# Mixing stage and MLP: high weight parts times high and low activation parts in one 512-column matmul, the two halves of the bank added at eviction

## The chip, the cores and the metric

The kernel runs as one program on one core of a Trainium2 chip. The metric is the device time of one execution in microseconds (us). The kernel before was timed three times. One more execution was recorded by the hardware profiler, and all rows below come from that one. In the text TensorE is PE, its weight loads are PEld, VectorE is DVE, ScalarE is ACT, GpSimd is POOL and SyncE, which issues most DMAs, is SP.

## The reference

One decoder layer on 256 tokens of width 1024, all in fp32:

```python
h = rmsnorm(x, g_pre_mix)
cb, cc, cv, q, k, v, qm, ga, gb, gc = split(h @ w_in)        # 7 x 512 and 3 x 1024 columns
y_a = (cb * causal_dwconv(cc * cv, conv_mix_w)) @ w_conv_out
y_b = moba_attention(heads(q), heads(k), heads(v), rel_bias) @ w_attn_out   # 8 heads of 64, causal
y_c = memory_attention(qm, rmsnorm(mem, g_mem), w_mem_kv) @ w_mem_out       # 4 heads of 128, 256 tokens
merged = sigmoid(ga + b0) * y_a + sigmoid(gb + b1) * y_b + sigmoid(gc + b2) * y_c
x = x + rmsnorm(merged @ w_out, g_post_mix)
h = rmsnorm(x, g_pre_ffn)
a, g = split(causal_dwconv(h @ w_up, ffn_conv_w, ffn_conv_b))               # 2 x 2816 columns
x = x + rmsnorm((gelu(a) * g) @ w_down, g_post_ffn)
```

## The kernel before

**Products in parts.** Every fp32 operand of a large product is split into a high part, rounded to fp32r (a 4-byte type that PE streams in one pass), and a low part, the remainder. A product is the sum of three: high times high, high weight times low activation, low weight times high activation. Weights arrive by DMA on SP into `raw` (1 MB, three buffers). `split_until` makes the parts of a *piece* of 128x1024 numbers: ACT writes `wh` (line 191), DVE writes `wl` (line 192). There are five buffers of pieces, and a piece is split three pieces before PE uses it. Activations are kept transposed, as `hT`, `cT`, `oT`, `omT` and `h2T`, each with a high and a low half: index 0 and 1 of the second axis.

**Blocks.** `blocks` computes 128 output columns for all 256 tokens: the result has the columns on the partitions and the 256 tokens along the bank. `mm_cols` (lines 205 to 210) issues three matmuls of 256 columns for every 128 rows of the weights (a *k-tile*): 8 k-tiles for products with `hT` and `h2T`, 4 for those with `cT`, `oT`, `omT`. Two blocks share one PSUM bank, and an `evac` function then takes both at once. `bank` has four buffers (tag `mm`), `acc` four more for long accumulations.

**Stages.** After the memory branch's keys and values, the mixing stage runs the blocks of q and k (`q_evac`, `k_evac`), then attention heads with the generator `fill` between them: memory q, the short convolution's C, V and B (`conv_evac`), and the 24 steps of `merges`, where `gate` turns two blocks into tanh values and `branch` multiplies two blocks of a branch's output by them. Then comes the output product `po` with `w_out`, with 512-column matmuls whose moving operand is the weight part (`mm_ktile`, line 216). `residual` normalises and adds (`post_norm`), turns the sum `x1` with PE transposes, and makes `h2T`. In the MLP, `up` computes two blocks of the gate half and two of the other half for each of eleven chunks, scales them by the second norm's factor `r2s`, convolves, applies GELU and splits the result `f`; the product with `w_down` accumulates in `pf` by line 216, one chunk behind. The factor depends on the token, which lies along the free axis of a block, so it is spread over all partitions by a matmul of `ones` with a diagonal (`diagonals`, `spread`).

**Order.** Each engine works its queue in order. A scheduler orders the instructions by due times while the program is built. In `residual`, in the first chunk and at the very end (`manual_schedule`), the order is that of the code. `both_blocks` does the first two blocks of the MLP with all high activation parts first.

Of the kernel before, what the change touches and what calls it, by code (L numbers as in the profile page):

```python
# [19 lines left out]
P = 128  # L20
# [35 lines left out]
def trunk(ctx, tc, x, mem, rel_bias, g_pre_mix, g_post_mix, g_pre_ffn, g_post_ffn, g_mem, w_in, b_gate,  # L56
# [235 lines left out]
    def blocks(nb, a, evac):  # L292

        p, wh, wl = None, None, None
        for b in range(nb):
# [11 lines left out]
            yield  # L307

    def both_blocks(a):

        ws = [weights(hold=i > 0) for i in range(2)]
        d = [p[:, :S] for p in acc("ft")]
        for k in range(KT):
            for i, (wh, wl) in enumerate(ws):
                nc.tensor.matmul(d[i], wh[:, k], a[:, 0, k], start=(k == 0), stop=False)
                nc.tensor.matmul(d[i], wl[:, k], a[:, 0, k], start=False, stop=False)  # L316
        for i, (wh, _) in enumerate(ws):
            for k in range(KT):
                nc.tensor.matmul(d[i], wh[:, k], a[:, 1, k], start=False, stop=(k == KT - 1))  # L319
        return d  # L320

    def run(gen):
        for _ in gen:
            pass

    def to_parts(dst, scale=1.0):
        return lambda b, p: hilo(dst[:, 0, b:b + 2], dst[:, 1, b:b + 2], two(p), scale)

# [114 lines left out]
    def q_evac(b, p):  # L443
        for j, r in enumerate(HEAD):
            hi, src = q2[r, b:b + 2, j], two(p)[r]
            nc.scalar.activation(hi, src, AF.Copy, scale=DH ** -0.5)
            nc.vector.scalar_tensor_tensor(q2[HEAD[1 - j], b:b + 2, j], src, DH ** -0.5, f32(hi), op0=ALU.mult,
                                           op1=ALU.subtract)

    def k_evac(b, p):  # L450
        for j, r in enumerate(HEAD):
            hi, src = k2[r, b:b + 2, j], two(p)[r]
# [96 lines left out]
    def conv_evac(b, p):  # L549
        y = wk.tile([P, 2, S], F32, tag="y", name="y", bufs=YB)  # L550
        for i in range(2):
            nc.scalar.activation(y[:, i], z[:, b + i], AF.Copy, scale=cw[:, 8 + b + i:9 + b + i])
            conv_tail(y[:, i], z[:, b + i], cw[:, b + i:b + i + 1], cw[:, 4 + b + i:5 + b + i])
        nc.vector.tensor_tensor(y, two(p), y, ALU.mult)
        hilo(cT[:, 0, b:b + 2], cT[:, 1, b:b + 2], y)
# [3 lines left out]
    def gate(q, n):  # L559
        sg = wk.tile([P, 2 * S], F32, tag="y", name="sg", bufs=YB)  # L560
        merged[q, n] = sg

        def evac(b, p):
            for i in range(2):
                c = 8 * n + 2 * q + i
                nc.scalar.activation(sg[:, i * S:(i + 1) * S], p[:, i * S:(i + 1) * S], AF.Tanh, scale=0.5,
                                     bias=bgh[:, c:c + 1])

        return blocks(2, hT, evac)

    def branch(q, n):
        def evac(b, p):
# [4 lines left out]
            if n == 2:  # L577
                mg = merged["mg"]
                hilo(mg[:, 0, 2 * q:2 * q + 2], mg[:, 1, 2 * q:2 * q + 2], two(total), 0.5)

        return blocks(2, (cT, oT, omT)[n], evac)

    def fill():
        yield from blocks(4, hT, to_parts(qm))
        yield from blocks(4, hT, lambda b, p: nc.scalar.activation(z[:, b:b + 2], two(p), AF.Copy))
        yield from blocks(4, hT, lambda b, p: nc.vector.tensor_tensor(z[:, b:b + 2], two(p), z[:, b:b + 2], ALU.mult))
        yield from blocks(4, hT, conv_evac)
        merged["mg"] = sb.tile([P, 2, KT, S], F32R, tag="C", name="mg")
# [64 lines left out]
    def residual():  # L653
# [17 lines left out]
        r2.append(rstd_full(x1[:, 1], "r2"))  # L671
        dg2.append(diagonals(r2))


    def up(c, f, b0):
# [3 lines left out]

        def evac(half, u, p):  # L680
            v = wk.tile([P, 2, S], F32, tag="y", name="v", bufs=YB)[:, :n]
            if not r2s:
                r2s.append(spread(dg2[0], "r2s"))
# [13 lines left out]
        for half in (1, 0):  # L697
            u = wk.tile([P, 2 * S], F32, tag="y", name="u", bufs=YB)[:, :n * S]
            res.append(u)
            if c == 0 and half:  # L700
                late.append((half, u, both_blocks(h2T)))
                continue
            for _ in blocks(n, h2T, lambda b, p: late.append((half, u, p))):
                for item in late:
                    evac(*item)
                late.clear()
        g, a = res
# [69 lines left out]
```

## Time and profile before

| | |
|---|---|
| three timed runs | 461.5, 462.3, 462.58 us; median 462.3 us |
| the profiled execution | 459.3 us, of which the profiler's span is 457.5 us |
| granted TensorE clock over the span | 0.998 of 2.4 GHz |
| HBM read | 80.91 MB, 179 GB/s over the span |

The span is the time from the first to the last instruction in the trace; 1.8 us lie around it. The trace's own time lies 3.0 us under the median of the timed runs. A matmul row's duration reaches to its modelled end and overlaps the next rows, so the pace of PE is read from the distance between starts.

### The profile page before, as it was taken

The page shows a single profiled execution, that of the slowest core. Times are in us where ns is not written, and L with a number is a line of the kernel's source. Part 1 is how long each engine was busy: PE and PEld are TensorE (multiplying, and loading weights), DVE is VectorE, ACT ScalarE, POOL GpSimd, SP SyncE. Part 2 cuts the span into 40 slices and gives each one's busy share as a digit, 9 for nine tenths or more (in the row PEclk, how much of TensorE's full clock was granted, in tenths as well). Part 3 has the DMA queues.
Part 4 walks back from the last instruction along what each step waited for, and adds up shares of the span by engine and source line. Part 5 has one row for each costly group of instructions (what it writes and reads, how often), then busy time and mean ns, then how long its engine had stood idle before and what let it go on. Part 6 is the DMA issues. An engine that isn't in the chain of part 4 may idle for free.

```text
span 457.5 us, 8130 instructions
## 1 busy us (share of the span) xinstructions
PE 447.3 (98%) x3263; PEld 422.5 (92%) x3263; DVE 329.7 (72%) x524; ACT 259.1 (57%) x419; POOL 17.6 (4%) x45
## 2 busy tenths in 40 slices
PE   8999999999999999999999899999999999999993
PEld 5798999999999999999998699989999999999982
DVE  4696769759766676495466579987787787787864
ACT  5976556547465555454445467665565565565641
POOL 3330000000000000000000200000000000000001
PEclk9999999999999999999999999999999999999999
DMA  8989654544626526545958136555555555635402
GB/s 252 358 273 300 213 183 141 176 152 132 192 87 198 171 64 213 184 140 185 332 194 263 41 134 234 186 185 185 184 185 183 185 185 184 188 134 144 180 1 93
DMA packets 67890, 82.50 MB, mean 180 GB/s; under 512 B 2064, under 2 KB 60914, under 8 KB 67852
## 3 DMA queue, kind: packets, MB, share of 16 engines
q1 hardware_dynamic: 67100, 79.73, 52.5%
q0 software_dynamic: 464, 1.20, 0.9%
q10 hardware_dynamic: 288, 1.05, 0.7%
q8 instruction: 25, 0.41, 0.4%
q14 instruction: 13, 0.11, 0.1%
HBM read 80.91 MB, written 1.06 MB: 179 GB/s over the span
## 4 chain that ended last, share of the span: by engine, by line
PE 93%; DMA 3%; DVE 1%; issue 1%; ACT 1%; POOL 0%; SPq 0%; POOLq 0%; DVEq 0%; ACTq 0%
PE ft L210 21%; PE ft L209 21%; PE ft L208 21%; PE pf L216 13%; PE po L216 5%; PE pmv L216 2%; DMA raw<-in_w_in_dram 2%; PE pv L216 2%; PE po L221 2%; PE tp L272 1%; PE at L221 1%; DMA rows<-in_g_mem_dram 1%; DVE wl L192 0%; PE ft L319 0%; PE ft L316 0%
## 5 line engine op out<-in xcount | busy, mean ns | idle before, releaser
L191 ACT ACTIVATE wh<-raw 128x1024 fp32r<-128x1024 f32 (+1 forms) x147 | 151.4, 1035 | 152.5 <-PE ft L209 105.0
L192 DVE TENSOR_TENSOR wl<-raw,wh 128x1024 fp32r<-128x1024 f32 (+1 forms) x147 | 174.9, 1195 | 79.1 <-ACT wh L191 77.6
L210 PE MATMUL ft<-hT,wl 128*128 128x256 f32 x384 | 108.6, 283 | 0.0
L209 PE MATMUL ft<-hT,wh 128*128 128x256 f32 x384 | 108.6, 283 | 0.0
L208 PE MATMUL ft<-hT,wh 128*128 128x256 f32 x384 | 108.6, 283 | 0.0
L208 PE MATMUL ft<-h2T,wh 128*128 128x256 f32 x328 | 92.9, 283 | 0.0
L210 PE MATMUL ft<-h2T,wl 128*128 128x256 f32 x328 | 92.8, 283 | 0.0
L209 PE MATMUL ft<-h2T,wh 128*128 128x256 f32 x328 | 92.8, 283 | 0.0
L210 PEld LDWEIGHTS ft<-hT,wl 128*128 128x128 f32 x384 | 73.7, 192 | 0.1
L209 PEld LDWEIGHTS ft<-hT,wh 128*128 128x128 f32 x384 | 73.6, 192 | 0.1
L208 PEld LDWEIGHTS ft<-hT,wh 128*128 128x128 f32 x384 | 73.6, 192 | 0.1
L208 PEld LDWEIGHTS ft<-h2T,wh 128*128 128x128 f32 x328 | 62.9, 192 | 0.4
L209 PEld LDWEIGHTS ft<-h2T,wh 128*128 128x128 f32 x328 | 62.9, 192 | 0.3
L210 PEld LDWEIGHTS ft<-h2T,wl 128*128 128x128 f32 x328 | 62.9, 192 | 0.1
L216 PE MATMUL pf<-wh,f 128*128 128x512 f32 x176 | 49.2, 390 | 0.0
L216 PEld LDWEIGHTS pf<-wh,f 128*128 128x128 f32 x176 | 32.3, 188 | 6.1
L216 PE MATMUL pf<-wl,f 128*128 128x512 f32 x88 | 27.5, 390 | 0.0
L694 ACT ACTIVATE u<-v,fw 128x256 f32<-128x256 f32 x44 | 24.0, 589 | 4.0 <-DVE v L686 4.0
L688 DVE TENSOR_TENSOR v<-ft,r2s 128x512 f32<-128x512 f32 (+1 forms) x23 | 14.8, 644 | 10.5 <-PE ft L210 10.5
L216 PEld LDWEIGHTS pf<-wl,f 128*128 128x128 f32 x88 | 16.5, 188 | 3.6
L547 DVE SCALAR_TENSOR_TENSOR u<-v,fw,u 128x254 f32<-128x254 f32 x44 | 19.7, 478 | 0.1
L546 DVE SCALAR_TENSOR_TENSOR u<-v,fw,u 128x255 f32<-128x255 f32 x44 | 19.5, 478 | 0.3 <-ACT u L694 0.3
(190 smaller groups left out, 618.4 us busy)
## 6 DMA issues: line engine op xcount, KB each, us to landing
raw<-in_w_in_dram SPq DMA_DIRECT2D x24, 1024.0 KB, 5.1
raw<-in_w_up_dram SPq DMA_DIRECT2D x20, 1024.0 KB, 5.2
raw<-in_w_down_dram SPq DMA_DIRECT2D x22, 512.0 KB, 3.3
raw<-in_w_out_dram SPq DMA_DIRECT2D x8, 512.0 KB, 5.2
raw<-in_w_mem_kv_dram SPq DMA_DIRECT2D x8, 256.0 KB, 6.2
raw<-in_w_mem_kv_dram SPq DMA_DIRECT2D x2, 1024.0 KB, 8.2
raw<-in_w_in_dram SPq DMA_DIRECT2D x4, 512.0 KB
raw<-in_w_conv_out_dram SPq DMA_DIRECT2D x4, 512.0 KB
```

The source lines that it names most:

```text
L191: nc.scalar.activation(hi, v, AF.Copy)
L192: nc.vector.tensor_tensor(lo, v, f32(hi), ALU.subtract)
L208: nc.tensor.matmul(dst, wh[:, k], ah[:, k], start=(k == 0), stop=False)
L209: nc.tensor.matmul(dst, wh[:, k], al[:, k], start=False, stop=False)
L210: nc.tensor.matmul(dst, wl[:, k], ah[:, k], start=False, stop=(k == kt - 1))
L216: nc.tensor.matmul(d, a, w[:, c:c + 512], start=(first and w is wh and a is ah), stop=(last and a is al))
L221: nc.tensor.matmul(dst, a[i], b[j], start=(first and n == 0), stop=(last and n == 2))
L272: nc.tensor.transpose(p[:, t * P:(t + 1) * P], src[:, t, k * P:(k + 1) * P], ident)
L546: nc.vector.scalar_tensor_tensor(t[:, 1:], src[:, :S - 1], w1, t[:, 1:], op0=ALU.mult, op1=ALU.add)
L547: nc.vector.scalar_tensor_tensor(t[:, 2:], src[:, :S - 2], w0, t[:, 2:], op0=ALU.mult, op1=ALU.add)
L688: nc.vector.tensor_tensor(v, two(p)[:, :n], twice(r2s[0])[:, :n], ALU.mult)
L694: nc.scalar.activation(d, v[:, i], AF.Identity, bias=bb, scale=w2)
```

## The change

- `mm_wide` replaces `mm_cols` in all blocks but those of the memory keys. For each k-tile it issues one matmul of 512 columns, `wh` against the high and the low activation part (two runs of 256 columns, 8 k-tiles apart in SBUF, or 4), and one of 256 columns, `wl` against the high part, into the first half of the bank. A block now fills a bank, and two blocks no longer share one.
- `add_up` evicts a block: ACT copies the second half of the bank to SBUF (`t`, two buffers; in the MLP tag `e`, four buffers), then DVE adds the first half to it. The `evac` functions now read that sum in SBUF. C's blocks go straight into `z`; `gate` works in place; `branch` needs a buffer of tag `y` that it did not need before.
- The second norm's factor of the first 128 tokens is multiplied into `xs` before the transposes, a copy of `x1` scaled per partition. So after eviction only the other 128 tokens are multiplied by `r2s`, in SBUF, and the diagonal and its spreading matmul are needed for one token tile.
- `both_blocks` puts the products with low activation parts into the second half of its banks. The tile `rows` moves into `misc`, the diagonals share the buffer of `junk`.

```diff
+    def mm_wide(p, wh, wl, a):
+        kt = wh.shape[1]
+        for k in range(kt):
+            nc.tensor.matmul(p, wh[:, k], a[:, :, k], start=(k == 0), stop=False)
+            nc.tensor.matmul(p[:, :S], wl[:, k], a[:, 0, k], start=False, stop=(k == kt - 1))
+
+    def add_up(dst, p, tag="t", bufs=2):
+        t = wk.tile([P, S], F32, tag=tag, name="t", bufs=bufs)
+        nc.scalar.activation(t, p[:, S:], AF.Copy)
+        nc.vector.tensor_tensor(dst, p[:, :S], t, ALU.add)
...
+    def wide_blocks(nb, a, evac, dst=None):
+        y, wh, wl = None, None, None
+        for b in range(nb):
...
+            p = bank("ft")
+            mm_wide(p, wh[:, :, at:at + P], wl[:, :, at:at + P], a)
...
+            if b % 2 == 0:
+                y = wk.tile([P, 2, S], F32, tag="y", name="y", bufs=YB) if dst is None else dst[:, b:b + 2]
+            add_up(y[:, b % 2], p)
+            if b % 2:
+                evac(b - 1, y)
+            yield
...
-                nc.tensor.matmul(d[i], wh[:, k], a[:, 1, k], start=False, stop=(k == KT - 1))
+                nc.tensor.matmul(d[i][:, S:], wh[:, k], a[:, 1, k], start=False, stop=(k == KT - 1))
...
-        yield from blocks(4, hT, lambda b, p: nc.scalar.activation(z[:, b:b + 2], two(p), AF.Copy))
-        yield from blocks(4, hT, lambda b, p: nc.vector.tensor_tensor(z[:, b:b + 2], two(p), z[:, b:b + 2], ALU.mult))
+        yield from wide_blocks(4, hT, lambda b, y: None, z)
+        yield from wide_blocks(4, hT, lambda b, y: nc.vector.tensor_tensor(z[:, b:b + 2], y, z[:, b:b + 2], ALU.mult))
...
+        xs = wk.tile([P, 1, D], F32, tag="pT", name="xs", bufs=2)
+        nc.vector.tensor_scalar_mul(xs[:, 0], x1[:, 0], r2[0])
         for k in range(KT):
-            turn(tps[k], x1, 0, k)
+            turn(tps[k], xs, 0, k)
...
-            if isinstance(p, list):
-                for i in range(n):
-                    nc.vector.tensor_tensor(v[:, i], p[i], r2s[0], ALU.mult)
-            else:
-                nc.vector.tensor_tensor(v, two(p)[:, :n], twice(r2s[0])[:, :n], ALU.mult)
+            for i, p in enumerate(ps_):
+                add_up(v[:, i], p, "e", EB)
+            vt = v[:, :, P:]
+            nc.vector.tensor_tensor(vt, vt, r2s[0][:, None, :].broadcast_to([P, n, P]), ALU.mult)
```

**How it moves instructions.** The first place is PE's queue at the end of the product with `w_out`: `po00` and `po01` are the two halves of the first token tile, `po10` and `po11` those of the second. Before, the last rows of the first tile and the first two of the second:

```order
L216 MATMUL po00_2907<-wl_2980,mg_1575 128x512
L216 MATMUL po00_2907<-wh_2979,mg_1575 128x512
L216 MATMUL po01_2908<-wh_2963,mg_1575 128x512
L216 MATMUL po01_2908<-wh_2979,mg_1575 128x512
L216 MATMUL po01_2908<-wl_2980,mg_1575 128x512
L216 MATMUL po01_2908<-wh_2979,mg_1575 128x512
L216 MATMUL po10_2909<-wh_2929,mg_1575 128x512
L216 MATMUL po11_2910<-wh_2929,mg_1575 128x512
```

The same place now, again up to the first rows that belong to the second tile alone:

```order
L229 MATMUL po10_2700<-wh_2720,mg_1474 128x512
L229 MATMUL po00_2698<-wl_2755,mg_1474 128x512
L229 MATMUL po01_2699<-wl_2755,mg_1474 128x512
L229 MATMUL po00_2698<-wh_2754,mg_1474 128x512
L229 MATMUL po00_2698<-wh_2770,mg_1474 128x512
L229 MATMUL po01_2699<-wh_2754,mg_1474 128x512
L229 MATMUL po01_2699<-wh_2770,mg_1474 128x512
L229 MATMUL po11_2701<-wh_2720,mg_1474 128x512
L229 MATMUL po10_2700<-wl_2721,mg_1474 128x512
L229 MATMUL po00_2698<-wl_2771,mg_1474 128x512
L229 MATMUL po01_2699<-wl_2771,mg_1474 128x512
L229 MATMUL po11_2701<-wl_2721,mg_1474 128x512
```

Three matmuls of the second tile now stand ahead of the first tile's last ones; 24 used to follow, 21 do now.

The second place is DVE's queue in `residual`, from the norm of the second token tile on (`yo` is the row times the gain, `x1` the sum, `dg` the diagonal). Before:

```order
L619 TENSOR_TENSOR yo_3088<-po11_2910,gains_2904 128x512
L622 SCALAR_TENSOR_TENSOR x1_3019<-yo_3088,ro_3099,x_sb_72 128x256 x2
L622 SCALAR_TENSOR_TENSOR x1_3019<-yo_3088,ro_3099,x_sb_72 128x512
L669 SCALAR_TENSOR_TENSOR h2T_3020<-tp_3076,par_96,h2T_3020 128x256 x2
L669 SCALAR_TENSOR_TENSOR h2T_3020<-tp_3077,par_96,h2T_3020 128x256 x2
```

And now:

```order
L690 TENSOR_SCALAR xs_2871<-x1_2810,r2_2839 128x1024
L648 TENSOR_TENSOR yo_2881<-po10_2700,gains_2695 128x512
L648 TENSOR_TENSOR yo_2881<-po11_2701,gains_2695 128x512
L651 SCALAR_TENSOR_TENSOR x1_2810<-yo_2881,ro_2892,x_sb_72 128x256 x2
L651 SCALAR_TENSOR_TENSOR x1_2810<-yo_2881,ro_2892,x_sb_72 128x512
L700 SCALAR_TENSOR_TENSOR h2T_2811<-tp_2867,par_95,h2T_2811 128x256 x2
```

The scaling of the first tile, which waits for its second norm factor, stands ahead of the second tile's two rows `yo`, which stood behind no such wait.

The third place is DVE's queue after the last block of the MLP (`v` the evicted block, `u` its convolution, line 709 the product of the two halves, `f` the low part of the result, of which the second is needed by PE's last matmuls). Before, from the eviction of the last block, ft_5024:

```order
L688 TENSOR_TENSOR v_5049<-ft_5024,r2s_3242 128x256
L547 SCALAR_TENSOR_TENSOR u_4984<-v_5014,fw_855,u_4984 128x254
L227 TENSOR_TENSOR f_4905<-u_4944,f_4905 128x256
L546 SCALAR_TENSOR_TENSOR u_5019<-v_5049,fw_855,u_5019 128x255
L547 SCALAR_TENSOR_TENSOR u_5019<-v_5049,fw_855,u_5019 128x254
L709 TENSOR_TENSOR u_5019<-u_5019,u_4984 128x256
L227 TENSOR_TENSOR f_4983<-u_5019,f_4983 128x256
```

And now, from the eviction of the last block, ft_4634 (lines 578 and 579 are the convolution, 753 the product):

```order
L223 TENSOR_TENSOR v_4651<-ft_4634,t_4652 128x256
L578 SCALAR_TENSOR_TENSOR u_4599<-v_4621,fw_822,u_4599 128x255
L723 TENSOR_TENSOR v_4651<-v_4651,r2s_3048 128x128
L753 TENSOR_TENSOR u_4564<-u_4564,u_4531 128x256
L579 SCALAR_TENSOR_TENSOR u_4599<-v_4621,fw_822,u_4599 128x254
L578 SCALAR_TENSOR_TENSOR u_4629<-v_4651,fw_822,u_4629 128x255
L240 TENSOR_TENSOR f_4530<-u_4564,f_4530 128x256
L579 SCALAR_TENSOR_TENSOR u_4629<-v_4651,fw_822,u_4629 128x254
L753 TENSOR_TENSOR u_4629<-u_4629,u_4599 128x256
L240 TENSOR_TENSOR f_4598<-u_4629,f_4598 128x256
```

Ten rows stand from the last block's eviction to the last `f`, where seven stood, and the eviction itself waits for ACT's copy.

## Rows read from the trace of the kernel before

**Rows 1.** The page's first part: busy time of each engine, its share of the span, its instructions.

```profile
PE 447.3 (98%) x3263; PEld 422.5 (92%) x3263; DVE 329.7 (72%) x524; ACT 259.1 (57%) x419; POOL 17.6 (4%) x45
```

**Rows 2.** The longest entry in the list of PE's waits over the span: who was waited for, us in total, times, longest. The two entries that follow lie in the first 5 us.

```profile
PE tp L272 <- DVE x L622: 1.7, 2, 1.5
```

**Rows 3.** The groups of the first of the three matmuls of `mm_cols` (line 208) by activation, shape and count; behind the bar busy us and mean ns of one. The groups with cT and oT have 32 each, as the one with omT.

```profile
L208 PE MATMUL ft<-hT,wh 128*128 128x256 f32 x384 | 108.6, 283 | 0.0
L208 PE MATMUL ft<-h2T,wh 128*128 128x256 f32 x328 | 92.9, 283 | 0.0
L208 PE MATMUL ft<-omT,wh 128*128 128x256 f32 x32 | 8.9, 283 | 0.0
L208 PE MATMUL ft<-h2T,wx 128*128 128x256 f32 x8 | 2.3, 283 | 0.0
```

**Rows 4.** Timeline of PE in a chunk of the MLP: start, us, operation. The first three are `pf` matmuls of 512 columns in one unbroken stretch, the last two the second and the sixtieth of an unbroken run of 256-column matmuls.

```profile
339.73 1.07 PE L216 MATMUL pf<-wh,f 128*128 128x512 f32 x4
340.63 0.62 PE L216 MATMUL pf<-wl,f 128*128 128x512 f32 x2
341.09 1.07 PE L216 MATMUL pf<-wh,f 128*128 128x512 f32 x4
...
343.01 0.28 PE L209 MATMUL ft<-h2T,wh 128*128 128x256 f32 x1
...
349.97 0.28 PE L210 MATMUL ft<-h2T,wl 128*128 128x256 f32 x1
```

**Rows 5.** Timeline of PE at a head's output: six matmuls, three of 512 columns and three of 256 columns that write two separate runs of 128 columns of the bank, and the start of the next.

```profile
89.21 1.22 PE L221 MATMUL po<-pT,vk 128*128 128x512 f32 x6
90.26 0.28 PE L208 MATMUL ft<-hT,wh 128*128 128x256 f32 x1
```

**Rows 6.** Groups of instructions by line and shape, the nearest kin of those that the change adds: busy us, mean ns of one.

```profile
L566 ACT ACTIVATE sg<-ft,bgh 128x256 f32<-128x256 f32 x24 | 9.9, 464 | 0.1
L688 DVE TENSOR_TENSOR v<-ft,r2s 128x512 f32<-128x512 f32 x19 | 13.1, 690 | 9.9 <-PE ft L210 9.9
L688 DVE TENSOR_TENSOR v<-ft,r2s 128x256 f32<-128x256 f32 x4 | 1.7, 423 | 0.6 <-PE ft L210 0.6
L191 ACT ACTIVATE wh<-raw 128x1024 fp32r<-128x1024 f32 x139 | 146.6, 1059 | 148.5 <-PE ft L209 105.0 <-issue 15.8 <-PE pf L216 14.2
L192 DVE TENSOR_TENSOR wl<-raw,wh 128x1024 fp32r<-128x1024 f32 x139 | 169.5, 1224 | 77.0 <-ACT wh L191 75.6
L414 DVE TENSOR_SCALAR xn<-x_sb,rx 128x1024 f32<-128x1024 f32 x2 | 1.5, 752 | 0.8 <-POOL rx L244 0.8
```

**Rows 7.** Busy time of each engine in four stretches: from:to, length, busy us and instructions of PE, PEld, DVE, ACT and POOL, granted TensorE clock, DMA share, GB/s. They are attention with its filling, the merges, the first two chunks of the MLP, and its steady part.

```profile
70.00:140.00 70.00, 70.00 (x581) 69.61 (x580) 52.15 (x122) 41.10 (x81) 0.00 (x0) 1.00 0.45 145
140.00:237.00 97.00, 97.00 (x809) 96.87 (x809) 61.87 (x83) 50.02 (x83) 0.00 (x0) 1.00 0.57 189
268.00:303.00 35.00, 35.00 (x273) 34.02 (x272) 30.98 (x48) 22.26 (x31) 0.00 (x0) 1.00 0.61 209
303.00:439.00 136.00, 136.00 (x964) 128.34 (x963) 106.34 (x156) 77.42 (x106) 0.00 (x0) 1.00 0.51 171
```

**Rows 8.** The same four stretches for line 208 alone: one instruction is one k-tile of a block.

```profile
70.00:140.00 70.00, 47.43 (x168) 32.07 (x168) 1.00 0.45 145
140.00:237.00 97.00, 69.88 (x248) 47.37 (x248) 1.00 0.57 189
268.00:303.00 35.00, 22.40 (x79) 15.16 (x80) 1.00 0.61 209
303.00:439.00 136.00, 72.49 (x258) 49.28 (x257) 1.00 0.51 171
```

**Rows 9.** Timeline of `residual`: first DVE (`yo` of the second tile's two halves, then its `x1`), then PE's transposes of the first and of the second tile, then POOL's last step of the first tile's second norm factor `r` and of the second tile's first, `ro`. In square brackets the idle time before and who ended it.

```profile
258.56 0.69 DVE L619 TENSOR_TENSOR yo<-po,gains 128x512 f32<-128x512 f32 x1 [1.71 <-ACT junk L239]
259.92 0.69 DVE L619 TENSOR_TENSOR yo<-po,gains 128x512 f32<-128x512 f32 x1 [0.67 <-ACT junk L239]
260.91 1.54 DVE L622 SCALAR_TENSOR_TENSOR x<-yo,ro,x_sb 128x256 f32<-128x256 f32 x3 [0.30 <-POOL ro L244]
...
258.92 1.03 PE L272 MATMUL tp<-ident,x 128*128 128x128 f32 x8
261.45 0.83 PE L272 MATMUL tp<-ident,x 128*128 128x128 f32 x4 [1.50 <-DVE x L622]
...
258.17 0.57 POOL L244 TENSOR_TENSOR r<-ms,mhalf 128x1 f32<-128x1 f32 x1
...
260.31 0.57 POOL L244 TENSOR_TENSOR ro<-ms,mhalf 128x1 f32<-128x1 f32 x1
```

**Rows 10.** Timeline after the first blocks of the MLP: PE's spreading of the norm factor and the next matmul.

```profile
271.63 0.60 PE L260 MATMUL sp<-dg,ones 128*128 128x128 f32 x4
272.00 0.36 PE L208 MATMUL ft<-h2T,wh 128*128 128x256 f32 x1
```

**Rows 11.** Timeline of the end of the MLP: PE's first `pf` matmul after the last block and the row of four with the eighteenth behind that first one; DVE's eviction of the last block; ACT's high part of the last `f`.

```profile
439.31 0.63 PE L216 MATMUL pf<-wh,f 128*128 128x512 f32 x2
...
442.97 1.07 PE L216 MATMUL pf<-wh,f 128*128 128x512 f32 x4
...
439.51 0.42 DVE L688 TENSOR_TENSOR v<-ft,r2s 128x256 f32<-128x256 f32 x1
...
442.62 0.42 ACT L225 ACTIVATE f<-u 128x256 fp32r<-128x256 f32 x1 [0.49 <-DVE u L709]
```

More of the change, by code (lines that the diff above doesn't have):

```diff
@@ L451, in k_evac @@
         for j, r in enumerate(HEAD):
-            hi, src = k2[r, b:b + 2, j], two(p)[r]
+            hi, src = k2[r, b:b + 2, j], p[r]
             nc.scalar.activation(hi, src, AF.Copy)
@@ L455, in k_evac @@
             nc.vector.tensor_copy(k2[HEAD[1 - j], b:b + 2, j], f32(hi))
-    run(blocks(4, hT, q_evac))
-    run(blocks(4, hT, k_evac))
+    run(wide_blocks(4, hT, q_evac))
+    run(wide_blocks(4, hT, k_evac))
     fw = const.tile([P, 2, 4 * NFB], F32, name="fw")
@@ L578, in evac @@
                 mg = merged["mg"]
-                hilo(mg[:, 0, 2 * q:2 * q + 2], mg[:, 1, 2 * q:2 * q + 2], two(total), 0.5)
-        return blocks(2, (cT, oT, omT)[n], evac)
+                hilo(mg[:, 0, 2 * q:2 * q + 2], mg[:, 1, 2 * q:2 * q + 2], total, 0.5)
+        return wide_blocks(2, (cT, oT, omT)[n], evac)
     def fill():
-        yield from blocks(4, hT, to_parts(qm))
-        yield from blocks(4, hT, lambda b, p: nc.scalar.activation(z[:, b:b + 2], two(p), AF.Copy))
-        yield from blocks(4, hT, lambda b, p: nc.vector.tensor_tensor(z[:, b:b + 2], two(p), z[:, b:b + 2], ALU.mult))
-        yield from blocks(4, hT, conv_evac)
+        yield from wide_blocks(4, hT, to_parts(qm))
+        yield from wide_blocks(4, hT, lambda b, y: None, z)
+        yield from wide_blocks(4, hT, lambda b, y: nc.vector.tensor_tensor(z[:, b:b + 2], y, z[:, b:b + 2], ALU.mult))
+        yield from wide_blocks(4, hT, conv_evac)
         merged["mg"] = sb.tile([P, 2, KT, S], F32R, tag="C", name="mg")
@@ L671, in residual @@
         r2.append(rstd_full(x1[:, 1], "r2"))
-        dg2.append(diagonals(r2))
+        dg = wk.tile([P, P], F32, tag="junk", name="dg", bufs=1)
+        nc.vector.tensor_scalar_mul(dg, ident, r2[1])
+        dg2.append(dg)
     def up(c, f, b0):
@@ L678, in up, with evac @@
         res, late = [], []
-        def evac(half, u, p):
+        def evac(half, u, ps_):
             v = wk.tile([P, 2, S], F32, tag="y", name="v", bufs=YB)[:, :n]
             if not r2s:
-                r2s.append(spread(dg2[0], "r2s"))
-            if isinstance(p, list):
-                for i in range(n):
-                    nc.vector.tensor_tensor(v[:, i], p[i], r2s[0], ALU.mult)
-            else:
-                nc.vector.tensor_tensor(v, two(p)[:, :n], twice(r2s[0])[:, :n], ALU.mult)
+                p = bank("sp")
+                nc.tensor.matmul(p[:, :P], ones, dg2[0], start=True, stop=True)
+                r2s.append(const.tile([P, P], F32, tag="rs", name="r2s"))
+                nc.vector.tensor_copy(r2s[0], p[:, :P])
+            for i, p in enumerate(ps_):
+                add_up(v[:, i], p, "e", EB)
+            vt = v[:, :, P:]
+            nc.vector.tensor_tensor(vt, vt, r2s[0][:, None, :].broadcast_to([P, n, P]), ALU.mult)
             for i in range(n):
@@ L702, in up @@
                 continue
[L703 to L706, printed above, removed]
+            ps_, w = [], None
+            for i in range(n):
+                if w is None:
+                    w, at = weights(), 0
+                ps_.append(bank("ft"))
+                mm_wide(ps_[-1], w[0][:, :, at:at + P], w[1][:, :, at:at + P], h2T)
+                at += P
+                if at == w[0].shape[2]:
+                    w = None
+            late.append((half, u, ps_))
+            for item in late:
+                evac(*item)
+            late.clear()
         g, a = res
```

35 lines of the change are left out of this document (19 added, 16 removed).

## The prediction, made before the changed kernel was run

> **What bounds the kernel now.** I read the page's first part first: PE is busy for 447.3 of 457.5 us, and a chain of weight loads runs beside it [rows 1]. Busy is not yet bound, since a matmul row overlaps the next. So the second view is the list of PE's waits: the longest entry is 1.7 us, in `residual`, and the few others lie at the start [rows 2]. Between start and end PE has work nearly always, and the other engines are less than three quarters busy. What shortens PE's own stream shortens the kernel, as long as PE goes on not waiting.
>
> The third view is PE's pace. From 339.73 to 341.09 six matmuls of 512 columns start, 226.7 ns each. From 343.01 to 349.97 there are 58 steps of 256 columns in 6.96 us, 120.0 ns each [rows 4]. The difference of 106.7 ns for 256 columns is 2.4 columns a ns, the full clock; granted is 1.00 in every stretch [rows 7]. What remains at either width is 13.3 ns per matmul. Three matmuls of 256 take 360.0 ns, one of 512 and one of 256 take 346.7 ns: the columns are the same, one fixed cost is saved.
>
> The Trainium skill, in "TensorE: Matmul & The Clock Gate", section Back-to-back issue gap, gives N/2.4 + 2.5 ns for a warm isolated gap, 109.2 and 215.8 ns here. The trace disagrees, with 120.0 and 226.7 ns. By the page's 2.5 ns the term below would be 2.0 instead of 10.9 us.
>
> **PE's stream.** Line 208 ran for 384 k-tiles of `hT`, 328 + 8 of `h2T` and 3 x 32 of `cT`, `oT`, `omT` [rows 3]: 816 k-tiles, and each loses one matmul. 816 x 13.3 ns = **10.9 us saved**. The `memT` blocks and `both_blocks` keep their count. No row has a moving operand in two runs of 256. The bounds are 240 ns for it (two passes of 120.0 ns, nothing saved) and 226.7 ns (a matmul of 512 like `pf`). I take 226.7 ns, since six matmuls of which three write two runs take 1.05 us [rows 5], and 3 x 226.7 + 3 x 120.0 ns is 1.04 us: two runs cost nothing on the output side.
>
> The spreading of the norm factor took 0.37 us from its start to the next matmul's [rows 10], for four rows; one is left, **0.3 us saved**.
>
> **Eviction.** The 816 k-tiles make 114 blocks (48 + 42 of 8, 24 of 4), and two more come from `both_blocks`: 116 copies on ACT and 116 adds on DVE. Nearest to the copy is the tanh of 256 columns from PSUM, 464 ns; nearest to the add is the product of 256 columns with one operand in PSUM, 423 ns [rows 6]. That is 53.8 us on ACT and 49.1 us on DVE; the MLP's products from PSUM of 512 columns (690 ns) shrink to 256 columns in SBUF. None of it lies on PE's path while a bank is free in time. A block of 8 k-tiles takes 8 x 346.7 ns = 2.8 us, and with four banks three blocks lie between a bank's end and its next use: 8.3 us of cover, 4.2 us for blocks of 4. A copy behind one split on ACT and an add behind one split on DVE need 1.06 + 0.46 + 1.22 + 0.42 = 3.2 us [rows 6].
>
> So it depends on whether DVE keeps up in a stretch [rows 7, 8]. The k-tiles of a stretch give its blocks, and 13.3 ns each of PE time saved. Attention: 168 k-tiles are 21 blocks; 52.2 + 21 x 0.423 = 61.0 us in 70.0 - 2.2 us, 90%. Merges: 248 k-tiles, 24 blocks of 4 and 19 of 8; 61.9 + 43 x 0.423 = 80.1 us in 97.0 - 3.3 us, 85%. Steady MLP: 258 k-tiles, 32 blocks; 106.3 + 32 x 0.423 us, less 0.27 us (690 - 423 ns) for most of the 19 products of 512 columns [rows 6], some 115 us in 136.0 - 3.4 us, 87%. First chunks of the MLP: 79 k-tiles, 10 blocks and the two of `both_blocks`; 31.0 + 12 x 0.423 us, less some 1.6 us for smaller products, 34.5 us in 35.0 - 1.1 us. Only there is DVE full. Its work can spill into the next stretch, but the in-order queue holds adds behind splits, and the bank of the first whole block is given back only after the spread factor has been copied. I count the queue through: PE starts the fifth bank user about 0.3 us before that add ends. **0.3 us**, between 0 and 2.0 us. For attention I put **0.3 us**, between 0 and 3.0 us: DVE has 6.8 us to spare, but each softmax hangs on several steps in order. The merges and the steady MLP I put at nothing: three banks' time covers them; if that cover went, each late bank would cost PE what it is late.
>
> **`residual`.** PE's wait of 1.50 us comes from DVE's `x1` of the second tile [rows 9]. Now `xs` stands ahead of both `yo`. It needs the factor `r`, ready at 258.17 + 0.57 = 258.74 us; three matmuls of the second tile ahead of the first tile's end push it by 3 x 0.227 to 259.42 us. `xs` is kin to the 752 ns scaling of 1024 columns [rows 6]: until 260.2. Two `yo` of 0.69 us, started 0.60 apart, end at 261.45 instead of 260.61 us, and `x1`, which started at 260.91 for POOL's `ro`, starts at 261.45. **0.5 us lost**, between 0 (no push, then `yo` ends before `ro`) and 1.2 us. The transposes of the first tile start later by 1.3 us, inside the 1.5 us that PE waited anyway.
>
> **The end.** The first `pf` row after the last block starts at 439.31 us; the nineteenth, which needs the high part of the last `f`, at 439.31 + 18 x 0.227 = 443.39 us. It was ready at 442.62 + 0.42 = 443.04 us [rows 11]: 0.35 us to spare. Now the eviction is a copy (0.46 us) and an add (0.42 us) where one product of 0.42 us stood, then a product of 128 columns (some 0.3 us, an estimate from 423 ns at 256), and the DVE queue puts a convolution row of the block before between each two of these. Counted through by the order, from the block's end: the copy ends at 0.5, the add behind a convolution row at 1.3, the product behind another at 1.9, ACT's own step at 2.5, two convolution rows at 3.8, GELU at 4.3, the product of the halves at 4.75, the last high part at 5.2 us. It was 3.5 us before, and 0.35 us of that difference are to spare; the third `f`, due earlier, makes PE wait for some 0.3 us already, which is part of the same loss. **1.3 us lost**, between 0.5 (one step more on the chain, less the slack) and 1.9 us.
>
> **Sum.** -10.9 - 0.3 + 0.3 + 0.3 + 0.5 + 1.3 = -8.8 us. Against the trace's own 459.3 us (span 457.5 and 1.8 around it) that is 450.5 us. The three timed runs have a median of 462.3 us, 3.0 above it; against that it is **453.5 us**, which I give.
>
> **Rivals.**
> 1. *The fixed cost is not saved.* The two-run operand restarts at the border, or the 13.3 ns belong to something that stays. At 240 ns for the wide matmul nothing is saved, and the losses of 2.1 us (0.3 + 0.3 + 0.5 + 1.3, less 0.3) stay: 464.4 us. For it: no row shows such an operand. Against: the same 13.3 ns at both widths, and two runs at full pace on the output side. The Trainium skill, in "PSUM — Partial Sum Buffer", Specifications (TRN2), says that a non-contiguous pattern slows matmuls significantly; the two-run output of rows 5 disagrees. Chance 5%.
> 2. *Slower: banks come back late in the merges.* Blocks of 4 k-tiles leave 4.2 us of cover. With the gated product and the sum (512 columns, 0.69 us each) and both splits ahead, the way is 3.2 + 1.4 = 4.6 us. If that is the rule and a `y` buffer is waited for as well, each of the 24 branch blocks makes PE wait; at 0.5 us that is 12 us, 465.5 us. It decides from 9.7 us in all, 0.40 us per branch block. For it: DVE serves everything in order. Against: 85% load, and every second pair in the merges is a gate with 8 k-tiles, in which DVE catches up. Chance 7%.
> 3. *Short waits everywhere.* In each of the nine steady chunks, and in each attention head, PE waits some 0.3 us, because ACT's copies wait for PE and the next split stands behind them: 17 x 0.3 = 5 us more, 458.5 us. For it: ACT is now held between two blocks where it ran ahead before. Against: splits are three pieces, 8 us, ahead. Chance 14%.
>
> That the change doesn't do what it says is excluded: PE's new order holds 816 matmuls of each width.
>
> **How the numbers follow.** The forecast has 72%. It runs from 451.6 us (losses at their least, 0.5 us) to 457.0 us (all losses at their upper bounds, 2.0 + 3.0 + 1.2 + 1.9 = 8.1 instead of 2.4 us, would be 459.2; they will hardly all be met, and I allow some 60% of the way). The profiled execution lay 3.0 us under the median, so runs of the kernel can lie lower too, and the low end goes down to 450.5 us, the forecast against the trace's own time. The third rival reaches 458.5. The range of 450.5 to 458.5 us then leaves out rivals 1 and 2, 12%, and little else. A difference of 0.2% is about what a measurement of this kernel can tell from no change. Faster: the forecast and rival 3, 72 + 14 = 86%. Slower: rivals 1 and 2, 5 + 7 = 12%. The 2% that remain are waits of 8 to 10 us that eat the whole gain, the same within 0.2% (461.4 to 463.2 us).
>
> **What would show it.** Right: starts of 512 and 256 columns in turn, 346.7 ns for two; a group of 816 matmuls at 512 columns; PE busy near 436 us; PE's list of waits near 5 us, with entries at the last `f` and in `residual`. Wrong: a pair taking 360 ns (rival 1); waits of PE for DVE adds in the merges (rival 2) or by the dozen for banks or weight parts in the steady MLP (rival 3); a wait at the end well over 2 us.

## The result, and the profile after the change

The changed kernel is slower by 1.4%: the ratio to the kernel before is 1.0141, 95% interval 1.0092 to 1.019. Its executions took 466.76, 468.37 and 469.49 us against a median of 461.9 us (460.45 to 462.58) of the kernel before; a fourth execution of 739 us, with a granted clock of 0.556, is in no number here. The forecast was 453.5 us. The profiled execution took 466.76 us with a span of 465.0 us, 7.5 us more than before.

The page's first part of the changed kernel (engine, busy us, share of the span, instructions), against [rows 1]:

```profile
PE 443.7 (95%) x2445; PEld 380.3 (82%) x2445; DVE 360.2 (77%) x639; ACT 291.4 (63%) x533; POOL 19.6 (4%) x45
```

PE has 818 instructions less, as the change says, but is busy only 3.6 us less, and its share fell from 98 to 95%. So there are two questions: why the stream shrank so little, and what PE waits for.

The list of PE's waits of the changed kernel (who waits, for whom; us in total, times, longest), against [rows 2]:

```profile
PE sp L273 <- DVE dg L266: 6.9, 1, 6.9
PE pt L366 <- DMA misc<-in_g_mem_dram: 2.0, 1, 2.0
PE ft L216 <- DVE v L223: 1.7, 1, 1.7
PE tp L285 <- DVE xs L690: 1.5, 1, 1.5
PE pw L394 <- PEq L804: 0.8, 1, 0.8
PE pf L229 <- ACT f L238: 0.7, 1, 0.7
PE tp L285 <- DVE x L651: 0.7, 2, 0.4
```

The longest entry stands in the start, for which the prediction's sum has no term. PE needs the diagonals of the memory's norm factor there, `dg`, written by DVE. Timeline of the changed kernel, first DVE, then ACT, then PE:

```profile
26.65 2.35 DVE L191 TENSOR_TENSOR wl<-raw,wh 128x1024 fp32r<-128x1024 f32 x2
28.92 0.47 DVE L266 TENSOR_SCALAR dg<-ident,rm 128x128 f32<-128x128 f32 x2
...
18.85 0.63 ACT L252 ACTIVATE junk<-m_sb 128x512 f32<-128x512 f32 x1
...
27.09 0.62 ACT L252 ACTIVATE junk<-x_sb 128x512 f32<-128x512 f32 x1
27.61 0.20 ACT L252 ACTIVATION_READ_ACCUMULATOR junk<-x_sb 128x1 f32 x1
...
29.34 0.76 PE L273 MATMUL sp<-dg,ones 128*128 128x128 f32 x2 [6.89 <-DVE dg L266]
...
30.12 0.41 PE L208 MATMUL ft<-memT,wh 128*128 128x256 f32 x1
...
33.32 0.63 PE L273 MATMUL sp<-dg,ones 128*128 128x128 f32 x2
...
55.78 0.39 PE L229 MATMUL pv<-wh,hT 128*128 128x512 f32 x1
```

The factor `rm` hangs on the squares of `m_sb`, the last of which began at 18.85 us. But `dg` has now no buffer of its own: it takes the one buffer of `junk`, into which ACT writes all squares, and in the code those of `x_sb` stand between those of `m_sb` and `dg`. The last of them ends at 27.8 us, and `dg` comes behind it and two splits on DVE, the first begun at 26.65 us, at 28.92 us. PE stands for 6.89 us, and then starts the sixteen matmuls from 30.12 to 33.32 us 213.3 ns apart, where 256 columns took 120.0 ns in [rows 4]. The granted clock says why (windows of the changed kernel: from:to, length, busy us and instructions of PE, PEld, DVE, ACT, POOL, granted clock, DMA share, GB/s):

```profile
20.00:30.00 10.00, 3.11 (x14) 2.38 (x13) 7.79 (x10) 8.01 (x15) 4.98 (x8) 0.85 0.82 275
30.00:40.00 10.00, 10.00 (x72) 10.00 (x72) 4.81 (x7) 3.34 (x5) 0.93 (x2) 0.81 0.84 283
```

The clock falls during the wait, and PE then runs at the lower of its two levels, 1.2 GHz, until some 33.9 us. The Trainium skill, in "TensorE: Matmul & The Clock Gate", section Back-to-back issue gap, gives N/1.2 ns from start to start there, 213.3 ns for 256 columns, without the fixed cost of the higher level; the trace agrees. Fifteen steps cost 15 x 93.3 ns = 1.4 us more than at 2.4 GHz.

The end of the start, the last `pv` matmul, lies at 55.78 us. The same row of the kernel before:

```profile
47.20 0.39 PE L216 MATMUL pv<-wh,hT 128*128 128x512 f32 x1
```

So 8.6 us are lost ahead of the first block with a wide matmul. The wait, the clock and the 1.5 us by which the wait for the first small transfer grew (2.0 after 0.5 us) would be 9.8 us; some 1.2 us come back until then. Most of that is the kernel before's: around its first matmuls with `hT`, from 34 to 40 us, PE's steps are together some 0.8 us longer than such steps elsewhere, and in the changed kernel, which comes there later, they are not.

Second, the pace. Timeline of PE in the changed kernel's merges, an unbroken run of pairs:

```profile
200.76 0.40 PE L216 MATMUL ft<-hT,wh 128*128 128x512 f32 x1
201.00 0.28 PE L217 MATMUL ft<-hT,wl 128*128 128x256 f32 x1
...
205.71 0.40 PE L216 MATMUL ft<-hT,wh 128*128 128x512 f32 x1
```

Fourteen k-tiles in 4.95 us are 353.6 ns each, not 346.7. Over all starts from 60 to 446 us, waits left out, a wide step takes some 236 and a narrow one 117 ns, 353.4 together. The wide one is some 10 ns longer than forecast, the narrow one 3 ns shorter.

This mean hides two paces. In an earlier stretch of the same trace, in the same order, eleven pairs take 3.81 us, 346.4 ns each, as forecast:

```profile
99.17 0.39 PE L216 MATMUL ft<-hT,wh 128*128 128x512 f32 x1
...
102.98 0.39 PE L216 MATMUL ft<-hT,wh 128*128 128x512 f32 x1
```

Some 110 of 780 pairs run like that. In most other stretches three pairs take 1.06 us, 349, 350 and 361 ns in turn.

Third, the evictions. The groups of the new copies and adds (busy us, mean ns of one), against [rows 6]:

```profile
L222 ACT ACTIVATE t<-ft 128x256 f32<-128x256 f32 x116 | 42.2, 367 | 5.5 <-PE ft L217 5.4
L223 DVE TENSOR_TENSOR y<-ft,t 128x256 f32<-128x256 f32 x68 | 27.8, 417 | 1.5 <-ACT t L222 1.4
```

They cost less than their nearest kin (464 and 423 ns), and neither attention nor the merges have an entry in the list of waits. At the first blocks of the MLP there is one. Timeline of the changed kernel there, DVE, ACT, PE:

```profile
286.43 0.48 DVE L578 SCALAR_TENSOR_TENSOR u<-v,fw,u 128x255 f32<-128x255 f32 x1
...
287.86 0.48 DVE L579 SCALAR_TENSOR_TENSOR u<-v,fw,u 128x254 f32<-128x254 f32 x1
288.25 0.75 DVE L223 TENSOR_TENSOR v<-ft,t 128x256 f32<-128x256 f32 x2
...
285.16 1.08 ACT L729 ACTIVATE u<-v,fw 128x256 f32<-128x256 f32 x2
286.14 0.90 ACT L222 ACTIVATE t<-ft 128x256 f32<-128x256 f32 x3
...
288.82 0.47 PE L216 MATMUL ft<-h2T,wh 128*128 128x512 f32 x1 [1.71 <-DVE v L223]
```

The first two whole blocks were complete when PE went on behind them at 281.07 us. Their copies stand on ACT behind two steps of the convolution (`u`, line 729), their adds on DVE behind four more (lines 578 and 579). PE wants a bank at 287.1 us and gets it at 288.82, after the first of the two adds. By the distance between PE's starts, which also has the slow first step behind the wait, this costs 1.9 us.

### The profile page after: what moved, and what is told of

It reads as the page before. It is cut to its first block, busy times and chain, and to the rows that moved or that the text cites. A ratio compares the mean times of both kernels' runs of the same rounds, so it can differ in the third digit from the quotient of the medians.

```text
span 465.0 us, 6811 instructions
## 1 busy us (share of the span) xinstructions
PE 443.7 (95%) x2445; PEld 380.3 (82%) x2445; DVE 360.2 (77%) x639; ACT 291.4 (63%) x533; POOL 19.6 (4%) x45
## 3 DMA queue, kind: packets, MB, share of 16 engines
HBM read 80.91 MB, written 1.06 MB: 176 GB/s over the span
## 5 line engine op out<-in xcount | busy, mean ns | idle before, releaser
L216 PE MATMUL ft<-hT,wh 128*128 128x512 f32 x384 | 136.6, 398 | 0.0
L216 PE MATMUL ft<-h2T,wh 128*128 128x512 f32 x328 | 116.5, 399 | 1.7 <-DVE v L223 1.7
L216 PEld LDWEIGHTS ft<-hT,wh 128*128 128x128 f32 x384 | 72.1, 188 | 16.6
L216 PEld LDWEIGHTS ft<-h2T,wh 128*128 128x128 f32 x328 | 61.6, 188 | 17.2 <-issue 2.0
L217 PEld LDWEIGHTS ft<-hT,wl 128*128 128x128 f32 x384 | 72.5, 189 | 0.2
L222 ACT ACTIVATE t<-ft 128x256 f32<-128x256 f32 x116 | 42.2, 367 | 5.5 <-PE ft L217 5.4
L223 DVE TENSOR_TENSOR y<-ft,t 128x256 f32<-128x256 f32 x68 | 27.8, 417 | 1.5 <-ACT t L222 1.4
L255 POOL TENSOR_SCALAR se<-ss 128x1 f32<-128x1 f32 x10 | 3.8, 377 | 416.7 <-ACT junk L252 416.6
L223 DVE TENSOR_TENSOR v<-ft,t 128x256 f32<-128x256 f32 x44 | 18.1, 416 | 0.0
L229 PE MATMUL po<-wh,mg 128*128 128x512 f32 x64 | 17.8, 389 | 0.0
```

Source lines behind the costliest of these rows:

```text
L216: nc.tensor.matmul(p, wh[:, k], a[:, :, k], start=(k == 0), stop=False)
L217: nc.tensor.matmul(p[:, :S], wl[:, k], a[:, 0, k], start=False, stop=(k == kt - 1))
L222: nc.scalar.activation(t, p[:, S:], AF.Copy)
L223: nc.vector.tensor_tensor(dst, p[:, :S], t, ALU.add)
L229: nc.tensor.matmul(d, a, w[:, c:c + 512], start=(first and w is wh and a is ah), stop=(last and a is al))
L255: nc.gpsimd.tensor_scalar(se, ss[0], EPS, None, op0=ALU.add)
```

## The experiments

All are timed against the kernel before on their own chip; ratios have 95% intervals.

**e1: the diagonals with a buffer of their own.** It must come from another tag, since the memory that one more would take is not there.

```
-        dg = wk.tile([P, NT, P], F32, tag="junk", name="dg", bufs=1)
+        dg = wk.tile([P, NT, P], F32, tag="e", name="dg", bufs=EB)
```

> The changed kernel, but `diagonals` takes its tile from the four buffers of `e` instead of the one buffer of `junk`. Theory A (the start is lost to the shared buffer: DVE's `dg` waits for ACT's squares): PE's wait of 6.9 us for `dg` falls under 1 us, the granted clock from 20 to 40 us is 1.00 instead of 0.81 to 0.85, the last `pv` matmul starts near 48.7 us instead of 55.78 (before: 47.20; the 1.4 us of the late first transpose stay), and the ratio to the kernel before falls from 1.014 to about 1.000. Rival (the start is lost to something else, such as `rows` or the new order on the engines, and `dg` is only the place where it shows): the last `pv` stays behind 53 us and the ratio stays over 1.008.

Measured: 458.24 us, ratio 0.9961 (0.9944 to 0.9978). The wait for `dg` is gone, the clock from 20 to 40 us is 1.00, and the last `pv` starts at 48.84 us:

```profile
20.00:30.00 10.00, 10.00 (x75) 9.42 (x74) 7.81 (x10) 9.15 (x16) 4.67 (x10) 1.00 0.83 280
30.00:40.00 10.00, 9.98 (x71) 9.08 (x70) 8.69 (x13) 5.28 (x9) 2.17 (x3) 1.00 1.03 309
...
48.84 0.39 PE L229 MATMUL pv<-wh,hT 128*128 128x512 f32 x1
```

Theory A holds. One line turns a gain of 0.4% into a loss of 1.4%.

**e2: the kernel before with that one edit.**

```
-        dg = wk.tile([P, NT, P], F32, tag="dg", name="dg", bufs=1)
+        dg = wk.tile([P, NT, P], F32, tag="junk", name="dg", bufs=1)
```

> The kernel before with that one edit alone: `diagonals` shares the buffer of `junk`. Theory A: PE waits 5 to 8 us for `dg` near 22 us, the granted clock falls below 0.9 between 20 and 40 us, and the kernel is 6 to 9 us slower, ratio 1.013 to 1.020. Rival (the scheduler only reorders, and the wait belongs to the wide matmuls' kernel): a ratio within 0.997 to 1.003 and no wait for `dg` over 1 us.

Measured: 470.53 us, ratio 1.0222 (1.0201 to 1.0242), 10.3 us over the kernel before on this chip. The wait and the clock of the changed kernel are there without a single wide matmul:

```profile
PE sp L260 <- DVE dg L253: 6.9, 1, 6.9
```

The last `pv` starts at 55.81 us, beside 55.78. The price is above the expected 6 to 9 us: the granted clock was also 0.83 from 270 to 280 us in its profiled execution, behind PE's wait in `residual`, which the trace of the kernel before doesn't show.

**e3: `rows` with a tile of its own.**

```
-    rows, rows1, rows2, bk = misc[:8, :P], misc[:52, 896:], misc[:, P:3 * P].rearrange("p (a b) -> p a b", b=P), misc[:NB + 1, 512:512 + TOEP]
+    rows = wk.tile([P, 2, S], F32, tag="y", name="rows", bufs=YB)[:8, 0, :P]; rows1, rows2, bk = misc[:52, 896:], misc[:, P:3 * P].rearrange("p (a b) -> p a b", b=P), misc[:NB + 1, 512:512 + TOEP]
```

> The changed kernel, but `rows` has a tile of its own again (in a buffer of `y`) instead of a corner of `misc`. Theory B (the shared tile makes the transpose of the gains wait for more than its own transfer): PE's first transpose starts at 4.4 us instead of 5.93, its wait for a DMA is 0.5 instead of 2.0 us, and 0.5 to 1.5 us are won, ratio about 1.011. Rival (the transfer just landed later in that execution, as transfers do): the start stays between 4.4 and 6 us without a gain, ratio 1.012 to 1.016, since the wait for `dg` behind it ends when ACT's squares end.

Measured: 465.93 us, ratio 1.0127 (1.0106 to 1.0148); PE still waits 1.6 us for this transfer, and in e4, with the shared tile, 0.4 us. Theory B falls: the wait doesn't follow the tile.

**e4: the two parts of a k-tile side by side.** For hT, h2T, cT, oT and omT:

```
-    hT = sb.tile([P, 2, KT, S], F32R, tag="B", name="hT")
+    hT = sb.tile([P, KT, 2, S], F32R, tag="B", name="hT").rearrange("p k a s -> p a k s")
```

> The changed kernel, but hT, h2T, cT, oT and omT are laid out with the high and the low part of one k-tile side by side, so that the moving operand of 512 columns is one run. Theory C (the two runs of 256 cost the 7 ns by which a pair is slower than forecast): a pair of 512 and 256 columns takes 346.7 instead of 353 ns, 816 x 6.5 ns = 5.3 us are won, ratio about 1.003. Rival D (the pair is slow because widths alternate: a weight load finds only 256 columns to hide behind where 512 come next): 353 ns stay, ratio 1.012 to 1.016.

Measured: 466.09 us, ratio 1.0141 (1.011 to 1.0172). Timeline of PE in the merges:

```profile
199.76 0.40 PE L216 MATMUL ft<-hT,wh 128*128 128x512 f32 x1
...
205.41 0.40 PE L216 MATMUL ft<-oT,wh 128*128 128x512 f32 x1
```

Sixteen k-tiles in 5.65 us, 353.1 ns. Theory C falls: two runs of 256 columns cost the moving operand nothing. The Trainium skill's sentence that a non-contiguous pattern slows matmuls significantly ("PSUM — Partial Sum Buffer", Specifications (TRN2)) is of PSUM; for this operand, which lies in SBUF, the runs show no such price.

**e5 and e6: the same matmuls in another order**, on top of e1. In `mm_wide`, e5 first all wide, then all narrow; e6 two wide, two narrow in turn.

```
-        for k in range(kt):
-            nc.tensor.matmul(p, wh[:, k], a[:, :, k], start=(k == 0), stop=False)
+        for k in range(kt): nc.tensor.matmul(p, wh[:, k], a[:, :, k], start=(k == 0), stop=False)
+        for k in range(kt):
             nc.tensor.matmul(p[:, :S], wl[:, k], a[:, 0, k], start=False, stop=(k == kt - 1))
```

> The kernel of e1 (the diagonals with a buffer of their own), but in each block first all matmuls of 512 columns and then all of 256, the same matmuls and sums. Theory E (what a pair takes beyond 346.7 ns is the price of the two changes of width): eight wide ones start 227 to 232 ns apart and eight narrow ones 120 ns apart, a k-tile falls from 354.4 to about 347 ns, 816 x 7.7 ns = 6.3 us are won over e1, ratio about 0.983. Rival F (a wide matmul of this kind takes 237 ns wherever it stands): 237 + 118 ns stay, ratio 0.993 to 0.998. Either way the upper half of a bank is complete eight narrow matmuls, 0.96 us, before the block's end, so its copy can start before, and the waits at the first blocks of the MLP (1.7 us) and at the last f (0.7 us) may fall by up to 0.5 us each.

> The kernel of e1, but in the order wide, wide, narrow, narrow: half the changes of width. Theory E: half the price, a k-tile of about 350.5 ns, 3.1 us won over e1, ratio about 0.989. Rival F: 354 ns, ratio 0.993 to 0.998. A third outcome, that only the first wide matmul behind a narrow one is slow and not the narrow one behind a wide, shows in which of the four steps is the long one.

Measured: e5 454.52 us, 0.9848 (0.9821 to 0.9876); e6 455.99 us, 0.9878 (0.9849 to 0.9906). Timeline of PE in e6 (each row is a group of two):

```profile
201.49 0.63 PE L216 MATMUL ft<-hT,wh 128*128 128x512 f32 x2
201.96 0.39 PE L217 MATMUL ft<-hT,wl 128*128 128x256 f32 x2
...
205.67 0.63 PE L216 MATMUL ft<-hT,wh 128*128 128x512 f32 x2
```

Twelve k-tiles in 4.18 us, 348.3 ns; over the whole traces a k-tile takes some 348.7 ns in e6 and 349.0 in e5. Rival F falls: the same wide matmuls are faster in another order, by some 4.5 ns a k-tile. But theory E's rule, a price for each change of width, fails too: e6 has half the changes and is as fast a k-tile as e5, which has an eighth. Nor does alternation always cost. In e1 and in e8, which is the same kernel once more on another chip, the 112 pairs of the merges are the same instructions in the same order; timeline of PE in e1 and then in e8:

```profile
189.69 0.40 PE L216 MATMUL ft<-omT,wh 128*128 128x512 f32 x1
...
228.53 0.39 PE L216 MATMUL ft<-hT,wh 128*128 128x512 f32 x1
...
189.04 0.40 PE L216 MATMUL ft<-omT,wh 128*128 128x512 f32 x1
...
228.62 0.40 PE L216 MATMUL ft<-hT,wh 128*128 128x512 f32 x1
```

They take 38.84 us in e1, 346.8 ns a pair, and 39.58 us in e8, 353.4 ns. So one by one has two paces, and grouped has one between them. What decides between the two is not shown. What stays over 346.7 ns in e5 lies behind the change of width: the first five wide steps of a block take 233, 236, 229, 232 and 231 ns (means of 59 blocks), the last three 227, as for `pf`.

**e7: wide matmuls in the mixing stage alone**, on top of e1; `both_blocks`, `residual` and `up` are those of the kernel before.

> The kernel of e1 with the wide matmuls in the mixing stage alone; residual and MLP as before the change (three matmuls a k-tile, the factor of both tiles spread over the columns). By the traces the MLP's half of the change wins 336 x 5.6 ns = 1.9 us and 0.3 us for the factor, and loses 0.4 us in residual, 1.7 us at the first blocks and 0.7 us at the last f: a loss of 0.6 us. Theory G (these waits eat the MLP's gain): this kernel is 0.3 to 1 us faster than e1, ratio 0.994 to 0.996, its list of PE's waits has 1.7 us in residual, none at the first blocks and none at the end. Rival (the MLP's half pays, and the waits were there under other names): 2 us slower than e1, ratio 1.000 or more.

Measured: 457.06 us, ratio 0.9902 (0.9875 to 0.9929). Its list of PE's waits, in which the first blocks and the end of the MLP no longer stand:

```profile
PE tp L285 <- DVE x L651: 2.0, 2, 1.8
PE pt L366 <- DMA misc<-in_g_mem_dram: 1.5, 1, 1.5
PE pw L394 <- PEq L789: 0.8, 1, 0.8
```

The sign is theory G's. The gain over e1, 0.6%, is larger than the expected 0.3 to 1 us, on another chip. From the second tile's transposes to the last `pf` matmul e7 takes 188.55 us (258.81 to 447.36), the kernel before 188.54 (261.45 to 449.99), and e8, below, 189.25 (259.45 to 448.70): in these traces the MLP's half of the change loses 0.7 us. The rest of the gain over e1 is not traced.

**e8: e1 once more.**

> The kernel of e1 once more, now beside the two that follow. In e1's execution the granted clock was 0.83 from 260 to 270 us, behind PE's waits in residual, and that stretch and the MLP behind it took 1.7 us more than in the changed kernel's own trace. Theory H (the clock after these waits falls in some executions only, and it is what e1 lacks against e7): with a clock of 1.00 there, the way from the second tile's transposes to the last pf matmul is 188.7 us instead of 190.5, and the ratio is 0.991 to 0.994. Rival (the order of the instructions in e1 makes its MLP slower): 190.5 us and a ratio of 0.996 again, with the clock at 1.00.

Measured: 459.23 us, ratio 0.9961 (0.994 to 0.9983). The profiled execution had a clock of 1.00 from 260 to 270 us, and took 189.25 us for the stretch in which e1 took 190.47 (259.48 to 449.95): the fall of the clock costs 1.2 us. Expected were 188.7; the changed kernel's own trace has 189.45. The ratio did not move. Five of the twelve executions had a mean clock of 0.995 or more and took 457.3 to 458.1 us, seven had 0.989 to 0.993 and took 459.1 to 461.3 us. So theory H is right that the clock falls in some executions only. It is wrong that this is what e1 lacks against e7: six of e1's nine executions had a mean clock of 0.996 or more, and its ratio is 0.9961 as well.

**e9: the copies and adds of the MLP's first four blocks ahead of the rest**, on top of e1; `adds` holds the first lines of `evac`.

```
-            for item in late:
+            for item in [(half, u, adds(q)) for half, u, q in late]:
                 evac(*item)
```

> The kernel of e1, but in the first chunk of the MLP the copies and adds of all four blocks are issued ahead of the factor, the convolution rows and the rest. Theory I (the 1.7 us in which PE waits for DVE's add at the first blocks come from the order of the queues: the add that gives the bank back stands behind the convolution of the first half): that wait falls under 0.3 us, and 1 to 1.7 us are won over e8. Rival (DVE and ACT are simply full there, and the wait moves to the next bank): the list of PE's waits names another add near 290 us with 1 us or more, and the time is that of e8.

Measured: 456.79 us, ratio 0.9913 (0.9881 to 0.9945), 2.4 us under e8. Its list of PE's waits has no entry at the first blocks any more:

```profile
PE pt L366 <- DMA misc<-in_g_mem_dram: 2.0, 1, 2.0
PE tp L285 <- DVE xs L690: 1.5, 1, 1.5
PE pw L394 <- PEq L807: 0.8, 1, 0.8
PE pf L229 <- ACT f L238: 0.7, 1, 0.7
PE tp L285 <- DVE x L651: 0.4, 1, 0.4
```

Theory I holds: the wait came from the order of the queues, not from a full DVE. The gain of 2.4 us is above the expected 1 to 1.7.

**e10: e5 and e9 together.**

> e9 with the matmuls of a block grouped by width, as in e5: the version that the runs point to. Theories E and I together: 2.6 ns less for each of 816 k-tiles than e9, 2.1 us, and up to 0.9 us less than e5 (ratio 0.985): 0.982 to 0.985. Rival (the gain of e5 over e1 was the chip's clock in residual and the start, not the order): a ratio within 0.2% of e9's.

Measured: 453.18 us, ratio 0.9827 (0.98 to 0.9853), 3.6 us under e9 on the same chip, where 2.1 were expected; 816 x 4.3 ns (353.2 in e9's trace less 348.9) would be 3.5. The order of the matmuls is worth what its pace says. Timeline of PE in the merges, two blocks of eight k-tiles in 5.59 us, 349.4 ns each (the mean over the trace is 348.9):

```profile
200.37 2.00 PE L215 MATMUL ft<-hT,wh 128*128 128x512 f32 x8
202.22 1.11 PE L217 MATMUL ft<-hT,wl 128*128 128x256 f32 x8
...
205.96 1.09 PE L215 MATMUL ft<-omT,wh 128*128 128x512 f32 x4
```

**e11: e10 with the layout of e4.**

> e10 with the layout of e4 (the high and the low part of a k-tile side by side). Grouping by width left 348.8 ns for a k-tile, 2.1 ns over the forecast's 346.7. If that rest is the price of the two runs, hidden in e4 under the changes of width: a k-tile of 346.7 ns, 816 x 2.1 ns = 1.7 us less than e10, ratio about 0.979. If the two runs cost nothing at all: 348.8 ns stay and the ratio is 0.981 to 0.985.

Measured: 453.1 us, ratio 0.9846 (0.9831 to 0.9862); a k-tile takes 348.9 ns, as in e10. Two runs cost nothing in this order either.

## Why the prediction was wrong

The sum was -8.8 us; the traces differ by +7.5. By its own terms, in us:

| term | forecast | measured |
| --- | --- | --- |
| PE's stream | -10.9 | -5.4 (816 x 6.6 ns) |
| spread of the norm factor | -0.3 | -0.2 |
| attention, merges, steady MLP | +0.3 | 0, no wait |
| the MLP's first blocks | +0.3 | +1.9 |
| `residual` | +0.5 | +0.6 |
| the end | +1.3 | +1.3 |
| the start | no term | +8.6 |
| not traced | | +0.7 |

1. **The step that failed is a missing one.** The section on the change names that the diagonals share the buffer of `junk`; the sum has no term for it. The prediction read in [rows 2] that PE hardly waits and asked what each new instruction costs, but not what a buffer now waits for. All its working lies behind 70 us. A shared buffer is an added wait like any other: the next writer stands behind the last use of the buffer before it, here DVE's `dg` behind ACT's squares of `x_sb`, and PE behind `dg`. e2 shows this edit alone to cost 10 us, e1 its undoing to win 1.8% of the time. None of the rivals was it: rival 2 has the right sign, but its banks in the merges came in time.
2. **PE's stream was mis-sized.** That one fixed cost of 13.3 ns goes per k-tile is right in kind: some 110 pairs run at the forecast's 346.7 ns. Over all pairs the assumption "I take 226.7 ns" failed, since the mean is 353.4 ns and half of the 13.3 ns is lost again. The doubt that the prediction named, the two-run operand (rival 1), is refuted by e4 and e11. The loss goes with the order of the widths, and e5 and e6 win most of it back. The trace of the kernel before has a hint of it inside [rows 5]: the three wide steps there, behind narrow ones, take 234, 235 and 229 ns.
3. **The MLP's first blocks** were inside their bounds (0 to 2.0 us) but almost at the upper one. The step that failed is "I count the queue through: PE starts the fifth bank user about 0.3 us before that add ends": ACT's copy of that bank stood behind its own convolution steps, and DVE's add behind four rows, as e9 shows by moving them.
4. **`residual` and the end** were right in mechanism and size, within 0.1 us; attention and the merges were covered, as argued. From the first `pf` row after the last block to PE's last matmul the kernel before takes from 439.31 us [rows 11] to 449.99, 10.68 us, the changed one 11.98; the wait that its list names, 0.7 us, is only half of the loss. The last rows, of the kernel before and then of the changed one with its first:

```profile
449.99 0.39 PE L216 MATMUL pf<-wh,f 128*128 128x512 f32 x1
...
445.59 0.64 PE L229 MATMUL pf<-wh,f 128*128 128x512 f32 x2
...
457.57 0.39 PE L229 MATMUL pf<-wh,f 128*128 128x512 f32 x1
```

The spread has two rows left, not the one that the prediction counts.

Without the shared buffer the forecast would still have been too low by some 7 us: it wants 8.8 us less than the kernel before, and e1 has 1.8 less by its ratio of 0.9961. That is points 2 and 3. What stays open: 0.7 us of the traces' difference, of which 0.6 lie in the mixing stage, and what decides the pace of alternating widths.

## What to carry to other kernels

Read the allocation lines of a diff as dependencies: for each tile that changes its tag or pool, list who wrote and read the buffer last, where they stand in their engines' queues, and who waits for the new owner. A wait of PE costs its own length and, where the clock falls, the stretch at the lower level behind it (1.4 us behind `dg` here). When matmuls of two widths make one sum, try them grouped by width, which won 3.6 us here; and give back PSUM banks (copies and adds) before anything that only the next stage wants.

## What the runs showed that I had not expected

- Alternating 512 and 256 columns takes 346.7 or 353.4 ns a pair, by the stretch and by the execution, two and two 348.7, eight and eight 349.0; the columns alone are 320 ns.
- A moving operand of two separate runs goes as fast as one run: 353.6 and 353.1 ns a pair, 348.9 ns for both when grouped.
- The same wait of 1.5 us in `residual` is followed by a granted clock of 0.83 in e1 and 1.00 in e8, with the same instructions; it is worth 1.2 us.
